# First token group read by whole rows, turned on TensorE, and scaled on two other engines

## The chip, the cores and the metric

The kernel runs on one core of a Trainium2 chip. Its time is the device time of one execution in microseconds, the median of several runs. Five engines work side by side and each takes its own instructions in order: TensorE (PE; PEld is its weight load), VectorE (DVE), ScalarE (ACT), GpSimd (POOL) and SyncE (SP), which here only issues transfers. An engine waits only where an instruction needs the result of another engine or of a transfer.

## The reference, cut to what matters

One layer of a mixer over 2048 tokens of 1024 features, all in float32. The part that the change touches is the entrance of the layer:

```python
shift, scale, gate = jnp.split(jax.nn.silu(c) @ w_ada[l] + b_ada[l], 3, axis=-1)
h = rms_norm(x) * (1.0 + scale[:, None, :]) + shift[:, None, :]
y = h @ w_in[l]          # then split into retention and attention heads and their gates
```

`rms_norm` divides each token by the root of the mean of its 1024 squares. `scale` and `shift` are one number per feature. So every token needs its own factor, every feature its own factor and offset, and the factor of a token is known only when all of its 1024 features have been squared and summed. What follows (retention over chunks of 128 tokens, windowed attention with a sink, gating, output projection, a last norm) is the same before and after.

## The kernel before, in words

The 2048 tokens go in four groups of 512 (`GT`), and group 3 is the first. The 1024 features are eight rows of 128 (`NK = 8`, index `k`): a row lies on the 128 partitions, the 512 tokens beside one another, so that a row is at once the moving operand of the input projection. Float32 operands are split into a rounded high part and the rest as a low part, and each product is three matmuls (high x high, high x low, low x high; `PASSES`).

**The head.** Group 3 comes from HBM already with features on the partitions (`x3`, four transfers from `xt`). ACT squares the eight rows (L990), DVE adds the squares (`add`, L985), and four small matmuls sum them over the partitions (`own_sums`, L982). ACT makes the mean (L184), POOL the power -1/2 (L185), DVE a diagonal of it (L192), and PE spreads the token factors over all partitions into a bank `ps3` (L201). Beside this the row of `c` is copied to all partitions by two matmuls (`pc0`, L968) and passed through silu on ACT (`silu0`, L971). `warm` (L962) issues matmuls whose result nobody reads.

**The conditioning.** For each row `k`, `ada` loads two blocks of `w_ada` (`wss`, 512 KB each), multiplies each by the silu row and sums it (`weigh`, L216, 128x1024 on DVE), and adds the bias (L227): that gives shift and scale of the 128 features (`mod`).

**The first loop.** It runs over `k` from 0 to 7. `start_load` brings two rows of four column chunks of `w_in` every second `k` (L1030); ACT rounds them to the high part (L112), DVE subtracts to get the low part (`start_low`, L1042). `modulate` makes the row: DVE multiplies by the scale and by the token factor (L232), ACT adds the shift and rounds (`h3h`, L233), DVE takes the low part (`h3l`, L234). Then PE does 4 chunks x 2 halves x 3 passes = 24 matmuls for this row (L1069), into eight banks that stay open over all eight rows. For rows 1 to 7 the token factors are read from `r3`, a copy of `ps3` in SBUF (L1057).

The order on each engine is fixed by the program where `keep_in_program_order` (`fixed`) is used, by `behind(i)` (an instruction is issued after `i`), and otherwise by a scheduler. The `wss` blocks go round five buffers, the raw weights and other loads round seven.

## Time and profile before

| what | value |
|---|---|
| median of 3 runs | 1138.04 us (1137.48 to 1139.66) |
| the profiled execution | 1139.05 us, span 1137.2 us |
| PE busy | 1120.9 us (99% of the span) |
| DVE busy | 800.0 us (70%) |
| ACT busy | 466.9 us (41%) |
| POOL busy | 328.5 us (29%) |
| first matmul of the first loop | 18.77 us after the span's start |
| first matmul behind the first loop | 64.00 us |

A row of the timeline gives start, length, engine, line, operation, the tiles written and read, and how many instructions were merged; in square brackets the idle time ahead of it and what ended it. A line number is that of the kernel before. The span is the time from the first to the last instruction; the execution lasts 1.85 us longer.

### The profile page before, as it was taken

What the parts mean: (1) busy time and instruction counts of PE and PEld (TensorE: products, weight loads), DVE (VectorE), ACT (ScalarE), POOL (GpSimd) and SP (SyncE); (2) the same over time, 40 slices, a digit from 0 to 9 for tenths busy, and PEclk for the clock granted to TensorE, in tenths of its full rate; (3) what the DMA queues carried; (4) which work ended last, traced back from release to release, by engine and by line L of the source; (5) the groups of instructions that cost most, each with busy time, mean ns of one, the idle gap of its engine ahead of it and who ended that gap; (6) DMA issues with size and microseconds to landing.
All of it is one profiled execution on the core that took longest, in us unless ns stands there. A gap on an engine that the chain in (4) does not pass through costs nothing.

```text
span 1137.2 us, 18696 instructions
## 1 busy us (share of the span) xinstructions
PE 1120.9 (99%) x6342; PEld 961.7 (85%) x6342; DVE 800.0 (70%) x2033; ACT 466.9 (41%) x1032; POOL 328.5 (29%) x427
## 2 busy tenths in 40 slices
PE   8999999999999999999999999999999999999997
PEld 5886889989988889998888887888888888888886
DVE  7973994565763645756658266888888888888885
ACT  4344522242452002322110155555555555555563
POOL 0000020110010200000204154555555555555552
PEclk9998999999999999999999999999999999999999
DMA  9948893374675542534347267466666666666531
GB/s 339 337 150 254 293 284 134 118 264 117 191 238 166 158 123 75 169 110 143 93 148 251 70 180 252 162 226 229 225 229 228 228 227 227 227 227 227 190 140 74
DMA packets 156246, 219.59 MB, mean 193 GB/s; under 512 B 13043, under 2 KB 105075, under 8 KB 156022
## 3 DMA queue, kind: packets, MB, share of 16 engines
q1 hardware_dynamic: 140020, 210.30, 56.4%
q10 hardware_dynamic: 16130, 8.09, 2.4%
q8 instruction: 50, 0.82, 0.3%
q14 instruction: 46, 0.38, 0.1%
HBM read 130.13 MB, written 50.86 MB: 159 GB/s over the span
## 4 chain that ended last, share of the span: by engine, by line
PE 84%; DVE 5%; issue 5%; DMA 2%; ACT 2%; POOL 1%; POOLq 0%; DVEq 0%; ACTq 0%
PE pz L1313 14%; PE rv L357 8%; PE rk L344 8%; PE ag L344 7%; PE o L1232 6%; PE aq L344 5%; PE rg L344 4%; PE S L769 4%; PE rq L344 4%; PE pt L1215 4%; PE S L773 2%; PE u L473 2%; PE av L344 2%; PE ak L344 2%; PE y L834 1%
## 5 line engine op out<-in xcount | busy, mean ns | idle before, releaser
L796 POOL TENSOR_SCALAR p<-p,m 128x640 f32<-128x640 f32 (+1 forms) x112 | 95.2, 850 | 86.1 <-DMA kwin<-d_k 46.4
L1222 DVE TENSOR_TENSOR phl<-pt,phl 128x512 fp32r<-128x512 f32 x154 | 104.7, 681 | 20.6 <-ACT phl L1221 20.5
L786 ACT ACTIVATE p<-p,m 128x641 f32<-128x641 f32 (+1 forms) x112 | 92.3, 824 | 62.2 <-DVE m L783 40.4
L1221 ACT ACTIVATE phl<-pt 128x512 fp32r<-128x512 f32 x154 | 90.9, 592 | 40.2 <-PE pt L1215 33.8
L1313 PE MATMUL pz<-wg0h,mr 128*128 128x512 f32 (+1 forms) x264 | 99.9, 402 | 0.7 <-DVE mr L114 0.7
L1313 PE MATMUL pz<-wg1h,ma 128*128 128x512 f32 x240 | 94.6, 414 | 0.0
L777 DVE CUSTOM_DVE_ANT_0 p<-S,msk 128x640 f32<-128x640 f32 (+1 forms) x112 | 90.1, 805 | 2.9 <-PE S L773 1.1
L769 PE MATMUL S<-kwin,aq 128*128 128x384 f32 (+1 forms) x256 | 84.9, 351 | 0.4 <-DVE m L777 0.4
L449 ACT ACTIVATE vw<-v,wdec 128x128 fp32r<-128x128 f32 x128 | 43.7, 394 | 84.3 <-DVE v L462 84.2
L1232 PE MATMUL o<-phl,vwin 128*128 128x512 f32 x180 | 72.1, 428 | 0.2 <-ACT phl L1221 0.2
L773 PE MATMUL S<-kctx,aq 128*128 128x256 f32 x256 | 71.1, 281 | 0.0
L1215 PEld LDWEIGHTS pt<-identr,pr 128*128 128x128 f32 x552 | 60.0, 141 | 11.6 <-DMA pr<-p 0.8
L1215 PE MATMUL pt<-identr,pr 128*128 128x128 f32 x552 | 63.0, 241 | 0.4 <-DMA pr<-p 0.4
L1313 PEld LDWEIGHTS pz<-wg0h,mr 128*128 128x128 f32 x264 | 49.2, 188 | 9.5 <-DVE mr L114 0.9
L769 PEld LDWEIGHTS S<-kwin,aq 128*128 128x128 f32 x256 | 48.1, 188 | 5.4 <-DVE m L777 1.8
L773 PEld LDWEIGHTS S<-kctx,aq 128*128 128x128 f32 x256 | 48.3, 189 | 3.1
L1313 PE MATMUL pz<-wg0l,mr 128*128 128x512 f32 (+1 forms) x132 | 50.9, 385 | 0.0
L1313 PEld LDWEIGHTS pz<-wg1h,ma 128*128 128x128 f32 x240 | 45.2, 188 | 5.2
L1313 PE MATMUL pz<-wg1l,ma 128*128 128x512 f32 x120 | 47.2, 393 | 0.0
L1277 ACT ACTIVATE ob<-o 64x512 f32<-64x512 f32 x32 | 19.0, 595 | 67.4 <-PE o L1232 67.4
L451 DVE SCALAR_TENSOR_TENSOR vw<-v,wdec,vw 128x128 fp32r<-128x128 f32 x128 | 39.9, 357 | 6.7 <-ACT vw L449 6.7
L1232 PE MATMUL o<-phl,vctx 128*128 128x512 f32 x128 | 43.9, 405 | 0.0
(456 smaller groups left out, 3116.5 us busy)
## 6 DMA issues: line engine op xcount, KB each, us to landing
pr<-p SPq DMA_DIRECT2D x104, 320.0 KB, 3.0
wss<-in_wss SPq DMA_DIRECT2D x32, 512.0 KB, 6.4
...
```

The lines of the kernel that those rows point to most:

```text
L344: pe.matmul(ps, w[:, a, k, c0 : c0 + P], ht[b][:, k, :], start=(k == 0 and i == 0), stop=(k == NK - 1 and i == 2),)
L357: pe.matmul(ps, ht[a][:, k, t * P : (t + 1) * P], w[:, b, k, :], start=(k == 0 and i == 0), stop=(k == NK - 1 and i == 2),)
L769: i = pe.matmul(psc[:, o:512].rearrange("p (s t) -> p s t", t=P), AQ[b][:, h, :], C2["kwin"][:, kv, hl, ksel], start=(hl == 0), stop=(hl = ...
L773: pe.matmul(psc[:, 512:768], AQ[b][:, h, :], C2["kctx"][:, kv, hl], start=(hl == 0), stop=(hl == 1))
L777: i = PE["max"] = dve.tensor_tensor_reduce(out=pb[:, 0:n], in0=psc[:, o : o + n], in1=mk, op0=ALU.add, op1=ALU.max, scale=1.0, scalar=-3e3 ...
L786: act.activation(pb[:, 0 : n + 1], pb[:, 0 : n + 1], AF.Exp, bias=m4[:, 1, j : j + 1], scale=0.125, accum_out=m4[:, 2, j : j + 1],)
L796: PE["norm"] = pool.tensor_scalar(pb[:, 0:n], pb[:, 0:n], m4[:, 2, j : j + 1], 0.0, op0=ALU.mult, op1=ALU.add)
L1215: pe.transpose(ppt[:, j].bitcast(F32R), x, identr)
L1221: PE["phl"] = act.activation(phl[0], ppt, AF.Copy)
L1222: PE["low"] = dve.tensor_tensor(phl[1], ppt, phl[0], op=ALU.subtract)
L1232: pe.matmul(PO[kv], vt, PH[kt][hl], start=(kt == 0 and hl == 0), stop=(kt == nkt - 1 and hl == 1))
L1313: PE["prod"] = pe.matmul(pz, m[:, a, k % RH, :], WG[k // 4][c][:, k % 4, s], start=(k == 0 and i == 0), stop=(k == NK - 1 and i == 2),)
```

## The change

Only the head and the first loop are written anew.

- **Load.** Group 3 is read as four blocks of 128 tokens by 1024 features (`xr`, from `xn`), 512 KB each as before. PE turns it: 32 transposes of 128x128 (`turn`), and ACT copies the eight turned banks into `x3` (`turned`).
- **Squares.** A token is now one partition, so a square and its sum are one instruction for a block of 128x1024 (`square`): two on ACT, two on DVE, all ahead of the two silus. The seven adds and the summing matmuls are gone.
- **The row of c** lies in a tile that DVE has cleared first, and is copied out by matmuls over 128 partitions where it was one.
- **Diagonal.** Half of it is made on DVE between the two `weigh` of row 0, half on ACT.
- **Row 0** (`first_row`) has its order written out. Its weights come as half pieces (`start_load(0, 0)` and `start_load(0, 1)`, 128 KB each), and the low part of chunk rg1 is made on POOL.
- **Rows 1 to 7** (`later_row`): POOL multiplies the row by the token factors in place, ACT applies scale and shift in one instruction, ACT rounds, DVE subtracts. One DVE instruction per row (L232) is gone and the other (L234) becomes a plain subtraction; POOL has one more per row and ACT one more.

On **POOL**, around the head and the first loop (r_x: the power of the token means; wrg: weights of chunk rg; h2x: the group `x3`; r: the token factors `r3`; half: constants). Before:

```order
masks.py:197 MEMSET ident 128x128
masks.py:199 ISA
masks.py:199 AFFINE_SELECT ident<-ident 128x128
L185 TENSOR_TENSOR r_x_212<-r_x_212,half_84 128x4
L185 TENSOR_TENSOR r_x_587<-r_x_587,half_84 128x4
L185 TENSOR_TENSOR r_xc<-r_xc,half_84 128x2
```

Now:

```order
masks.py:199 AFFINE_SELECT ident<-ident 128x128
L1012 TENSOR_TENSOR r_x_198<-r_x_198,half_84 128x4
L1059 TENSOR_TENSOR wrg_236<-wr_s_0_251,wrg_236 128x256
L1088 TENSOR_TENSOR h2x_132<-h2x_132,r_247 128x512 x7
L185 TENSOR_TENSOR r_x_615<-r_x_615,half_84 128x4
L185 TENSOR_TENSOR r_xc<-r_xc,half_84 128x2
```

Where POOL had nothing between the powers of two groups, it now has a subtraction and seven multiplications one behind the other.

On **DVE**, from the low part of row 0 to the conditioning of row 2 (wss: blocks of `w_ada`; wrg, w_srq: weights; h3h, h3l: the row's parts). Before:

```order
L234 SCALAR_TENSOR_TENSOR h3l<-h2x_125,mod,h3h 128x512
L1042 TENSOR_TENSOR wrg_232<-wr_s_0_246,wrg_232 128x512
L216 SCALAR_TENSOR_TENSOR wss_1_0_286,acc_113<-wss_1_0_286,row_123 128x1024
L216 SCALAR_TENSOR_TENSOR wss_1_1_289,acc_113<-wss_1_1_289,row_123 128x1024
L227 TENSOR_TENSOR mod<-acc_113,nbada 128x2
L232 SCALAR_TENSOR_TENSOR h2x_125<-h2x_125,mod,r_257 128x512
L216 SCALAR_TENSOR_TENSOR wss_2_0_320,acc_113<-wss_2_0_320,row_123 128x1024
L234 SCALAR_TENSOR_TENSOR h3l<-h2x_125,mod,h3h 128x512
L216 SCALAR_TENSOR_TENSOR wss_2_1_323,acc_113<-wss_2_1_323,row_123 128x1024
L1042 TENSOR_TENSOR wrg_231<-wr_s_1_327,wrg_231 128x512
L227 TENSOR_TENSOR mod<-acc_113,nbada 128x2
```

Now (after `h3l` of row 0 and the low part of rq0):

```order
L209 SCALAR_TENSOR_TENSOR wss_1_0_295,acc_113<-wss_1_0_295,row_123 128x1024
L1059 TENSOR_TENSOR w_srq_237<-wr_s_0_251,w_srq_237 128x256
L209 SCALAR_TENSOR_TENSOR wss_1_1_298,acc_113<-wss_1_1_298,row_123 128x1024
L222 TENSOR_TENSOR mod<-acc_113,nbada 128x2
L1059 TENSOR_TENSOR wrg_235<-wr_s_0_248,wrg_235 128x256
L1059 TENSOR_TENSOR w_srq_238<-wr_s_0_248,w_srq_238 128x256
L1091 TENSOR_TENSOR h3l<-h2x_132,h3h 128x512
L1059 TENSOR_TENSOR w_srq_237<-wr_s_0_251,w_srq_237 128x256
L1059 TENSOR_TENSOR wrg_236<-wr_s_0_251,wrg_236 128x256
L209 SCALAR_TENSOR_TENSOR wss_2_0_342,acc_113<-wss_2_0_342,row_123 128x1024
L209 SCALAR_TENSOR_TENSOR wss_2_1_345,acc_113<-wss_2_1_345,row_123 128x1024
L1059 TENSOR_TENSOR wrg_235<-wr_s_1_349,wrg_235 128x512
```

The scaling of row 1 has left DVE, the weights come in halves, and both blocks of row 2 stand behind the low parts of row 1, where the first of them stood ahead of `h3l` of row 1. The sum of row 2 (`mod`) follows the last row shown.

The diff, cut to its core:

```diff
-    act.dma_start(row0[0:1], crow[0:1])
+    xr = [ld.tile([P, D], F32, tag="ld", name=f"xr3_{t}") for t in range(4)]
+    for t in range(4):
+        nc.sync.dma_start(xr[t], xn[(12 + t) * P : (13 + t) * P, :])
     x3 = half("h2x3", [P, NK, GT], F32)
-    for i in range(4):
-        nc.sync.dma_start(x3[:, 2 * i : 2 * i + 2], xt[3][:, 2 * i : 2 * i + 2])
...
+    dve.memset(row0, 0.0)
+    act.dma_start(row0[0:1], crow[0:1])
...
+    def square(t, eng):
+        y, a = sq[t % 2], s3.ss[:, t : t + 1]
+        if eng == "act":
+            fixed(act.activation(y, xr[t], AF.Square, accum_out=a))
+        else:
+            fixed(dve.scalar_tensor_tensor(y, xr[t], 1.0, xr[t], op0=ALU.mult, op1=ALU.mult, accum_out=a))
+    def turn(t, ks):
+        for k in ks:
+            fixed(pe.transpose(xp[k][:, t * P : (t + 1) * P], xr[t][:, k * P : (k + 1) * P], ident))
+    def turned(*ks):
+        for k in ks:
+            PE["turned"] = fixed(act.activation(x3[:, k], xp[k], AF.Copy))
...
+    warm(6)
...
+    turn(0, range(6))
+    for n in range(2):
+        fixed(pe.matmul(pc0[n], ones, row0[:, n * GT : (n + 1) * GT], start=True, stop=True))
+    for t in range(1, 4):
+        turn(t, range(6))
+    square(0, "act")
+    square(1, "dve")
+    square(2, "act")
+    square(3, "dve")
     silu0(0)
     silu0(1)
+    for t in range(4):
+        turn(t, (6, 7))
...
+    turned(0, 1)
+    warm(5, ps3)
...
+    ada(
+        st0, "ada", row0, 0, 0, fix=fixed,
+        between=lambda: fixed(dve.tensor_tensor(dg[:, 0:2], i2, r2_, op=ALU.mult)),
+    )
+    for t in (2, 3):
+        fixed(act.activation(dg[:, t], ident, AF.Copy, scale=r[:, 0, t : t + 1]))
+    for t in range(4):
+        fixed(pe.matmul(ps3[:, t * P : (t + 1) * P], ones, dg[:, t], start=True, stop=True))
+    turned(2)
+    warm(8, pacc.tile([P, GT], F32, tag="acc", name="warm2"))
...
+    def first_row():
+        x, h = x3[:, 0], H[3]
+        shk, sck = mod[:, 0, 0, 0:1], mod[:, 0, 0, 1:2]
+        start_high(0, CH[:1], 0, 1, fixed)
+        turned(3)
+        start_high(0, CH[1:2], 0, 1, fixed)
+        PE["scaled"] = fixed(dve.scalar_tensor_tensor(x, x, sck, ps3, op0=ALU.mult, op1=ALU.mult))
+        start_low(0, CH[:1], 0, 1, fixed)
+        fixed(act.activation(h[0][:, 0, :], x, AF.Identity, bias=shk))
+        fixed(dve.scalar_tensor_tensor(h[1][:, 0, :], x, shk, h[0][:, 0, :], op0=ALU.add, op1=ALU.subtract))
+        start_low(0, CH[1:2], 0, 1, fixed)
+        lows = [PE["low0"]]
+        turned(6, 7)
+        start_high(0, CH[2:3], 0, 1, fixed)
+        start_low(0, CH[2:3], 0, 1, fixed)
+        fixed(act.activation(r3, ps3, AF.Copy))
+        start_high(0, CH[3:], 0, 1, fixed)
+        lows.append(PE["low0"])
+        start_low(0, CH[3:], 0, 1, eng=pool)
+        turned(4, 5)
+        return lows
+    def later_row(k):
+        x, h = x3[:, k], H[3]
+        with behind(plow):
+            pool.tensor_tensor(x, x, r3, op=ALU.mult)
+        act.activation(x, x, AF.Identity, bias=mod[:, k, 0, 0:1], scale=mod[:, k, 0, 1:2])
+        PE["hirow"] = act.activation(h[0][:, k, :], x, AF.Copy)
+        PE["row"] = dve.tensor_tensor(h[1][:, k, :], x, h[0][:, k, :], op=ALU.subtract)
...
     for k in range(NK):
-        if k:
-            ada(st0, "ada", row0, k, 0, (PE["scaled"],) * 2)
...
-        modulate(x3[:, k], r3 if k else ps3, 0, H[3], k)
...
+        if k == 0:
+            start_load(0, 0)
+            lows = first_row()
+        else:
+            cond = ada(st0, "ada", row0, k, 0, lows if k == 1 else (PE["row"],) * 2)
...
+            later_row(k)
```

More of the change, by code (lines that the diff above doesn't have):

```diff
@@ L219, in behind, with ada @@
         return tc.issue_after(i.ins) if i else nullcontext()
-    def ada(pl, tag, row, kc, which, after=(None, None)):
+    def ada(pl, tag, row, kc, which, after=(None, None), fix=lambda i: i, between=lambda: None):
         for j in range(2):
@@ L225, in ada @@
             with behind(after[j](i) if callable(after[j]) else after[j]):
-                i = weigh(w, row, acc2[:, kc, which, j : j + 1])
+                i = fix(weigh(w, row, acc2[:, kc, which, j : j + 1]))
+            if j == 0:
+                between()
         return dve.tensor_tensor(mod[:, kc, which], acc2[:, kc, which], nbada[:, kc:16:8], op=ALU.add)
@@ L964, in tile_hymba @@
     fixed = tc.keep_in_program_order
-    warm(12)
-    for n in range(2):
-        pc0[n] = ptp.tile([P, GT], F32, tag="tp", name=f"pc0{n}")
-        fixed(pe.matmul(pc0[n], ones[0:1], row0[0:1, n * GT : (n + 1) * GT], start=True, stop=True))
     def silu0(n):
@@ L973, in tile_hymba @@
     s3 = Stats(GT, "x3")
-    zero4 = rsm.tile([P, 4], F32, tag="zero", name="zero4", bufs=1)
-    dve.memset(zero4, 0.0)
-    s3.ss = ptp.tile([P, 4], F32, tag="tp", name="ss_x3")
-    fixed(pe.matmul(s3.ss, ones, zero4, start=True, stop=False))
-    def own_sums(x):
-        for t in range(4):
-            fixed(pe.matmul(s3.ss[:, t : t + 1], x[:, t * P : (t + 1) * P], ones[:, 0:1], start=False, stop=t == 3))
-    def add(x, y):
-        fixed(dve.tensor_tensor(x, x, y, op=ALU.add))
-    sq = [tmp(f"sq_x3_{k}") if k < 4 else ld.tile([P, GT], F32, tag="ld", name=f"sq_x3_{k}") for k in range(NK)]
@@ L989, in square @@
-    def square(k):
-        fixed(act.activation(sq[k], x3[:, k], AF.Square))
-    warm(12)
-    for i in range(2):
-        square(2 * i)
-        square(2 * i + 1)
-        add(sq[2 * i], sq[2 * i + 1])
-    add(sq[0], sq[2])
-    square(4)
-    square(5)
-    add(sq[4], sq[5])
-    add(sq[0], sq[4])
-    square(6)
+    s3.ss = rsm.tile([P, 4], F32, tag="ss", name="ss_x3")
+    def square(t, eng):
[4 more added lines that the diff above has]
+            fixed(dve.scalar_tensor_tensor(y, xr[t], 1.0, xr[t], op0=ALU.mult, op1=ALU.mult, accum_out=a))
@@ new lines, in turn @@
+    def turn(t, ks):
[4 more added lines that the diff above has]
+            PE["turned"] = fixed(act.activation(x3[:, k], xp[k], AF.Copy))
+    sq = half("h2sq", [P, 2, 2 * D], F32)[:, :, 0:D]
+    sq = [sq[:, i] for i in range(2)]
+    warm(6)
+    for n in range(2):
+        pc0[n] = ptp.tile([P, GT], F32, tag="tp", name=f"pc0{n}")
+    xp = [
+        (ptp if k > 4 else pacc).tile([P, GT], F32, tag="tp" if k > 4 else "acc", name=f"xp{k}") for k in range(NK)
+    ]
@@ L1003, in tile_hymba @@
+    turn(0, range(6))
+    for n in range(2):
+        fixed(pe.matmul(pc0[n], ones, row0[:, n * GT : (n + 1) * GT], start=True, stop=True))
[5 more added lines that the diff above has]
+    square(3, "dve")
     silu0(0)
-    square(7)
-    add(sq[0], sq[6])
     silu0(1)
-    add(sq[0], sq[7])
-    own_sums(sq[0])
-    warm(8)
-    s3.roots(ada(st0, "ada", row0, 0, 0))
-    ps3 = s3.spread()
-    warm(6)
+    for t in range(4):
+        turn(t, (6, 7))
```

72 lines of the change are left out of this document (42 added, 30 removed).

## The prediction

> **What bounds the kernel now.** I read the page's totals first, then the waits of PE in the first 75 us, then the timeline of each engine there.
>
> ```profile
> PE 1120.9 (99%) x6342; PEld 961.7 (85%) x6342; DVE 800.0 (70%) x2033; ACT 466.9 (41%) x1032; POOL 328.5 (29%) x427
> ...
> PE frg L1069 <- ACT h3h L233: 0.6, 2, 0.3
> PE aq L344 <- ACT g L604: 0.3, 1, 0.3
> ```
>
> PE is the bound of the whole, and once the first loop runs it hardly waits: 0.6 us for the parts of a row, 0.3 us ahead of the next projection. So the change can gain only by starting the loop sooner, and can lose by making PE wait inside it; both pass to the end one for one. The rows that set the start, and those that set row 2:
>
> ```profile
> 8.86 0.63 ACT L990 ACTIVATE sq_x<-h2x 128x512 f32<-128x512 f32 x1
> ...
> 11.92 1.22 DVE L216 SCALAR_TENSOR_TENSOR wss<-wss,row 128x1024 f32<-128x1024 f32 x1
> ...
> 13.20 0.27 ACT L184 ACTIVATE r_x<-ss_x,half 128x4 f32<-128x4 f32 x1 [2.08 <-PE ss_x L982]
> 13.55 1.63 POOL L185 TENSOR_TENSOR r_x<-r_x,half 128x4 f32<-128x4 f32 x1 [12.26 <-ACT r_x L184]
> 15.21 0.69 DVE L192 TENSOR_TENSOR dg_x<-ident,r_x 128x512 f32<-128x512 f32 x1 [0.72 <-POOL r_x L185]
> 16.05 1.13 PE L201 MATMUL rr_x<-dg_x,ones 128*128 128x128 f32 x8 [1.14 <-DVE dg_x L192]
> 17.22 0.75 DVE L232 SCALAR_TENSOR_TENSOR h2x<-h2x,mod,rr_x 128x512 f32<-128x512 f32 x1 [0.71 <-PE rr_x L201]
> 18.00 0.72 ACT L233 ACTIVATE h3h<-h2x,mod 128x512 fp32r<-128x512 f32 x1 [2.18 <-DVE h2x L232]
> 18.77 0.73 PE L1069 MATMUL frg<-h3h,wrg 128*128 128x512 f32 x2 [0.30 <-ACT h3h L233]
> ...
> 27.27 0.15 DVE L227 TENSOR_TENSOR mod<-acc,nbada 128x2 f32<-128x2 f32 x1
> 27.34 1.28 DVE L1042 TENSOR_TENSOR w_srq<-wr_s,w_srq 128x512 fp32r<-128x512 f32 x2
> 28.54 0.68 DVE L1042 TENSOR_TENSOR wrg<-wr_s,wrg 128x512 fp32r<-128x512 f32 x1
> ...
> 30.70 0.73 PE L1069 MATMUL frg<-h3h,wrg 128*128 128x512 f32 x2 [0.33 <-ACT h3h L233]
> ...
> 64.00 0.50 PE L344 MATMUL aq<-h3h,w_s 128*128 128x512 f32 x1 [0.29 <-ACT g L604]
> ```
>
> The loop's first matmul is at 18.77. The last quarter of the input is there by 8.86 (its first square starts then); the ten microseconds between are sums, mean, power, diagonal, spread, scaling. Rows 2 to 7 take 64.00 - 0.29 - 30.70 = 33.0 us, or 5.5 each: from row 2 on PE sets the pace.
>
> ```profile
> 18.77:25.00 6.23, 6.13 (x26) 4.78 (x27) 6.08 (x12) 1.61 (x4) 0.00 (x0) 1.00 1.00 367
> 25.00:31.00 6.00, 5.67 (x25) 4.37 (x24) 6.00 (x12) 2.36 (x5) 0.00 (x0) 1.00 0.96 322
> ```
>
> Columns: the stretch, its length, busy time of PE, PEld, DVE, ACT, POOL, PE clock, share and GB/s of DMA. While rows 0 and 1 run DVE has no gap (6.08 of 6.23, 6.00 of 6.00) and POOL does nothing. DVE is the near second; whatever holds it up in rows 0 to 2 reaches PE.
>
> **The change, part by part. The head.** The four blocks bring the same bytes, so I keep 8.86 for the last. On its square DVE spends what a `weigh` of the same shape takes, 1.22: sums at 10.1. ACT's mean 0.27: 10.4. POOL's power 1.63: 12.1. ACT makes half of the diagonal, two pieces of 0.39: 12.9, while DVE makes the other half between the two `weigh`. The spread ends with its last matmuls at 13.6 (1.13 for eight from 12.5, when DVE's half is there). DVE meanwhile does the second `weigh` (12.5 to 13.7) and the sum (13.9); then L1068 and ACT's rounding, 0.75 and 0.72: first matmul at 15.4, **3.4 us sooner**. Seven adds, the summing matmuls and two squares behind one another are what is saved.
>
> The rows for the diagonal, the SP issues and the transposes:
>
> ```profile
> L196 ACT ACTIVATE dg_x<-ident,r_x 128x128 f32<-128x128 f32 x4 | 1.3, 391 | 1.1 <-POOL r_x L185 1.1
> ...
> 5.26 1.75 SPq L1030 DMA_DIRECT2D wr_s<-in_win x4
> ...
> 284.97 0.82 PE L433 MATMUL pk<-ident,m_rk 128*128 128x128 f32 x6
> ...
> 5.79 1.98 PE L968 MATMUL pc<-row,ones 1*128 1x512 f32 x4
> ```
>
> Six transposes take 0.82, 0.11 from start to start, so the 14 behind the last block take 1.5 and are done by 10.4, ahead of the power; without that cover they would cost the 1.5. The two matmuls for the row of c (1.98) are due only when both of ACT's squares are done, near 8.7; the later transfer of that row can slip 0.6 before DVE, which waits for the power until 12.1, feels it. Half-size weight pieces mean four more issues on SP; the four of before took 1.75, so up to 1.8 of SP time, between nothing and that, and I take nothing, because the blocks of row 2 are not used until far later (below).
>
> **The loop.** Per row DVE loses L232 (0.75); ACT and POOL have room. But POOL now works while DVE does, and the trace has stretches where both do:
>
> ```profile
> 154.67 1.63 DVE L216 SCALAR_TENSOR_TENSOR wss<-wss,room 128x1024 f32<-128x1024 f32 x1
> 156.23 0.08 DVE L216 DVE_READ_ACCUMULATOR wss<-wss,room 128x1 f32 x1
> 156.23 0.56 DVE L227 TENSOR_TENSOR mod<-acc,nbada 128x2 f32<-128x2 f32 x1
> ...
> 153.90 5.25 POOL L110 TENSOR_SCALAR w_brk<-wr_brk 128x512 fp32r<-128x512 f32 x4 [53.17 <-DMA wr_brk<-in_win]
> ...
> 608.22 6.18 DVE L658 TENSOR_TENSOR wg0l<-wf,wg0h 128x512 fp32r<-128x512 f32 x6
> ...
> 601.46 9.34 POOL L110 TENSOR_SCALAR wg0h<-wf 128x512 fp32r<-128x512 f32 x8 [13.57 <-DVE wf L646]
> ...
> 808.52 2.09 DVE L1338 SCALAR_TENSOR_TENSOR xb<-xb,rz,fw 128x512 f32<-128x512 f32 x2
> ...
> 808.13 0.73 POOL L1284 TENSOR_TENSOR ma<-mf,ma 128x256 fp32r<-128x256 f32 x1
> 808.84 1.24 POOL L796 TENSOR_SCALAR p<-p,m 128x640 f32<-128x640 f32 x1
> ...
> L1284 POOL TENSOR_TENSOR ma<-mf,ma 128x256 fp32r<-128x256 f32 x32 | 23.4, 730 | 2.7
> L817 POOL TENSOR_TENSOR qd<-qkv,decq 128x512 f32<-128x512 f32 x30 | 38.1, 1291 | 0.0
> L110 POOL TENSOR_SCALAR w_ark<-wr_ark 128x512 fp32r<-128x512 f32 x8 | 4.7, 618 | 51.6 <-PE rk L344 33.9 <-PE rq L344 17.8
> ```
>
> The same `weigh` takes 1.63 instead of 1.22 and the same sum 0.56 instead of 0.15, both 0.41 more, while POOL rounds 128x512 beside them; POOL's four take 5.25, though one alone takes 0.62. Six subtractions beside POOL take 6.18, where alone they start 0.60 apart (27.34 to 28.54 is two). So a DVE instruction with two SBUF inputs and a POOL instruction exclude one another and take turns, and each POOL instruction costs a busy DVE its own time less some 0.2. Behind a two-input POOL instruction it is the same: the L1338 at 808.52 and the next need 2.09 for two, and the first cannot begin in earnest before the 0.73 from 808.13 is over.
>
> A POOL multiplication of two 128x512 tiles takes 1.29, so it holds DVE for about 1.09; that pairing of shapes is not in the trace. From below the price is 0.41 (the one-input rows), from above 1.29 (all of it); I take 1.09, since the 128x256 form held DVE to its end. The subtraction on POOL (0.73) holds 0.53. All eight run in rows 0 to 2, because the seven multiplications wait for nothing but turned rows: 7 x 1.09 + 0.53 = **8.2 us** laid on DVE.
>
> [...]
>
> DVE's own work from the first matmul to the sum of row 2, by the new order: `h3l` 0.66 and 0.61, four `weigh` at 1.14, six half subtractions at 0.34 (half of 0.60 and a little), one whole 0.61, two sums 0.1: 8.7. With 8.2 the sum of row 2 is at 16.9 behind the first matmul, and none of that hides in a wait: DVE reaches `h3l` of row 1 about 0.5 after ACT has the row ready. ACT's two instructions (0.6 each, with the hand-over 1.3) make row 2 ready at 18.2, that is 15.4 + 18.2 = 33.6, against 30.70: **2.9 later**. Three more subtractions (1.8) and `h3l` (0.68) stand ahead of the low part, at 19.4; PE wants it 0.45 after its start and waits **0.75**. By the same turn-taking row 1 is late too (ready at 6.6, low part at 9.0, PE done with it at 13.9), which leaves PE idle for 4.3 us ahead of row 2.
>
> ```profile
> 8.00:8.50 0.50, 0.50 (x3) 0.19 (x3) 0.47 (x2) 0.50 (x2) 0.00 (x0) 0.53 1.07 410
> ...
> 11.00:11.50 0.50, 0.50 (x3) 0.15 (x1) 0.40 (x2) 0.12 (x1) 0.00 (x0) 0.56 0.99 348
> ...
> 15.00:16.00 1.00, 0.00 (x0) 0.00 (x0) 0.79 (x2) 0.76 (x2) 0.18 (x1) 1.00 1.04 426
> ```
>
> That has a price of its own: behind the two microseconds of matmuls over one partition (L968, above) the granted clock was 0.53 and less from 8.0 to 11.5. An idle stretch of 4.3 should do the same: 3.4 us at half clock lose 1.7. Bounds: nothing (the 1.14 ahead of L201 left it at 1.00), and twice that; I take **1.7**. From row 3 on DVE has 9.7 per two rows (four `weigh`, two `h3l`, four subtractions, sums, one wait for ACT) against PE's 11.0: no further wait, and no catching up, since PE is full. The 0.3 ahead of aq goes, as ACT has more time there.
>
> Sum: 2.9 + 0.75 + 1.7 - 0.3 = 5.05 us. The profiled execution took 1139.05 (span 1137.2): 1144.1. It stood 1.0 above the median of 1138.04, so against the median **1143.1**.
>
> **The rivals.**
>
> *The two engines do not exclude each other for these forms.* Then row 2 is ready at 15.4 + 8.7 + 1.3 and a wait of 1.2 in row 1, near 26.7, 4.0 sooner: 1134. For it: POOL's 30 multiplications in L817 keep 1.29 each beside a DVE that is 70% busy. Against: most of DVE's work there reads PSUM, and every DVE instruction of this loop reads two SBUF tiles.
>
> *The hold is that of the one-input rows*, 8 x 0.41 = 3.3 instead of 8.2. Then row 2 is at 28.7, 2.0 sooner, with no gap long enough to cool PE: 1138.04 - 2.0 - 0.3, near 1136. Against: L1284.
>
> *PE is cold in the head.* The clock row above shows how little it takes. If it is at half clock from 8 on, the five `warm` and the spread (1.13, doubled) end 1.8 later, and everything hangs on the spread: 1144.9. For it: six `warm` fewer at the start. Against: the row of c now uses all 128 partitions. [...]
>
> **How the numbers follow.** Forecast 0.55, cold head 0.12, short hold 0.16, no exclusion 0.17. What this kernel's runs can tell from no change is about 0.2%, or 2.3 us: below 1135.8 is faster, above 1140.3 slower. No exclusion is faster; of the short hold half is, half the same; the forecast without the clock term and with a little less hold gives 1140, so 0.06 of it goes to the same. Faster 0.24, same 0.15, slower 0.61. The range leaves out most of the no-exclusion case below and, above, two windows of half clock on a cold head: 1135.5 to 1147. The forecast's own range is 1140 to 1146.
>
> **What would show it.** First matmul of the loop near 15.4. In rows 0 to 2, DVE subtractions of 128x256 near 1.4 and `weigh` near 2.3 beside seven POOL multiplications of 1.6 to 2.4 that end near 31. A PE wait of over 3 us ahead of row 2, then a clock below 1.00. Row 2 at 33.6, the projection aq at 69. It is wrong if POOL's seven take 1.29 each and DVE's lengths stay as they were, or if row 2 starts before 30.7.

## The result, and the profile after

The changed kernel takes 1143.93 us (median of 6 runs, 1143.51 to 1145.88) where the kernel before takes 1137.86 (6 runs beside it): a ratio of 1.0054, with a 95% interval of 1.0041 to 1.0067, or 6.1 us more. Its profiled execution took 1145.88, with a span of 1144.1 (before: 1139.05 and 1137.2).

The waits of TensorE in the first 90 us after the change (what waited, for what: us in total, how often, the longest):

```profile
PE frg L1128 <- ACT h3h L1090: 5.5, 2, 3.2
PE pc L998 <- DMA row<-in_crow: 2.0, 1, 2.0
...
PE aq L339 <- ACT g L599: 1.2, 1, 1.2
PE frg L1128 <- DVE h3l L1091: 1.1, 1, 1.1
```

The 0.6 us of waits for a row's parts became 6.6, the wait ahead of aq went from 0.3 to 1.2, and there is a new one in the head, 2.0 for the row of c. The head, in the timeline of TensorE:

```profile
7.55 3.10 PE L998 MATMUL pc<-row,ones 128*128 128x512 f32 x4 [2.03 <-DMA row<-in_crow]
10.44 3.58 PE L982 MATMUL xp<-ident,xr 128*128 128x128 f32 x26
13.87 1.24 PE L962 MATMUL rr_x<-wones 128*128 128x512 bf16 x5
14.94 1.05 PE L1024 MATMUL rr_x<-dg_x,ones 128*128 128x128 f32 x8
17.59 0.73 PE L1128 MATMUL frg<-h3h,wrg 128*128 128x512 f32 x2
```

The loop starts at 17.59, 1.18 sooner than before. The four matmuls of the row of c start late and take 3.10 us, and 26 transposes stand behind them in TensorE's fixed order. Then the loop, in the timelines of GpSimd, of VectorE and of TensorE:

```profile
19.69 0.74 POOL L1059 TENSOR_TENSOR wrg<-wr_s,wrg 128x256 fp32r<-128x256 f32 x1 [6.25 <-DMA wss<-in_wss]
20.39 11.16 POOL L1088 TENSOR_TENSOR h2x<-h2x,r 128x512 f32<-128x512 f32 x7
```

```profile
18.58 1.22 DVE L209 SCALAR_TENSOR_TENSOR wss<-wss,row 128x1024 f32<-128x1024 f32 x1
...
19.72 0.99 DVE L1059 TENSOR_TENSOR w_srq<-wr_s,w_srq 128x256 fp32r<-128x256 f32 x1
20.63 2.31 DVE L209 SCALAR_TENSOR_TENSOR wss<-wss,row 128x1024 f32<-128x1024 f32 x1
...
22.99 1.11 DVE L222 TENSOR_TENSOR mod<-acc,nbada 128x2 f32<-128x2 f32 x1
24.02 0.41 DVE L1059 TENSOR_TENSOR wrg<-wr_s,wrg 128x256 fp32r<-128x256 f32 x1
24.36 1.48 DVE L1059 TENSOR_TENSOR w_srq<-wr_s,w_srq 128x256 fp32r<-128x256 f32 x1
...
30.32 2.31 DVE L209 SCALAR_TENSOR_TENSOR wss<-wss,row 128x1024 f32<-128x1024 f32 x1
...
34.31 0.15 DVE L222 TENSOR_TENSOR mod<-acc,nbada 128x2 f32<-128x2 f32 x1
```

```profile
36.09 1.22 PE L1128 MATMUL frg<-h3h,wrg 128*128 128x512 f32 x2 [3.23 <-ACT h3h L1090]
71.54 0.50 PE L339 MATMUL aq<-h3h,w_s 128*128 128x512 f32 x1 [1.20 <-ACT g L599]
```

GpSimd's seven multiplications take 11.16, that is 1.59 apart where one alone takes 1.29. From 20.6 to 31.5 VectorE's `weigh` takes 2.31 instead of 1.22 and the little sum L222 1.11 instead of 0.15; once GpSimd is done it takes 0.15 again (34.31). Seven of VectorE's instructions there are lengthened, one for each multiplication; those of them that don't stand above are low parts. The small one at 24.02 is not (0.41, its length alone). Such a hold shows as a longer instruction and not as idle time in square brackets, so an engine can lose time in more ways than by waiting for a result. Row 2 starts at 36.09, which is 18.5 behind the loop's first matmul (before: 11.93), and aq at 71.54, 7.54 later than before. The stretches around row 2 (length, busy time of PE, PEld, DVE, ACT, POOL, granted clock, DMA share, GB/s):

```profile
30.00:34.00 4.00, 2.86 (x13) 2.05 (x11) 4.00 (x6) 0.00 (x0) 1.55 (x2) 1.00 0.09 22
34.00:36.00 2.00, 0.00 (x0) 0.00 (x0) 2.00 (x5) 1.41 (x2) 0.00 (x0) 0.88 0.89 296
36.00:38.00 2.00, 1.91 (x5) 1.54 (x6) 2.00 (x5) 0.04 (x1) 0.00 (x0) 0.50 0.82 181
38.00:40.00 2.00, 2.00 (x8) 1.63 (x7) 1.32 (x5) 0.55 (x1) 0.00 (x0) 0.77 1.01 363
```

Behind the gap TensorE's clock is at half from 36 to about 39 (0.50, then 0.77 over 38 to 40). And the loads nearly stop from 30 to 34 (share 0.09): SyncE, which issues them, waits 9.3 us in one piece there for VectorE to be done with a block of `wss`, since VectorE, held up, frees no buffers.

### The profile page after: what moved, and what is told of

It is laid out like the page before. It is cut to its first block, busy times and chain, and to the rows that moved or that the text cites. A ratio compares the mean times of both kernels' runs of the same rounds, so it can differ in the third digit from the quotient of the medians.

```text
span 1144.1 us, 18738 instructions
## 1 busy us (share of the span) xinstructions
PE 1119.2 (98%) x6344; PEld 963.1 (84%) x6345; DVE 802.2 (70%) x2026; ACT 474.6 (41%) x1049; POOL 342.3 (30%) x435
## 4 chain that ended last, share of the span: by engine, by line
PE 83%; DVE 5%; issue 4%; DMA 4%; POOL 2%; ACT 1%; SPq 0%; POOLq 0%; DVEq 0%; ACTq 0%
PE pz L1372 15%; PE rv L352 8%; PE rk L339 7%; PE ag L339 7%; PE o L1291 7%; PE aq L339 5%; PE rg L339 4%; PE S L764 4%; PE rq L339 4%; PE pt L1274 4%; PE S L768 2%; PE u L468 2%; PE av L339 2%; PE ak L339 2%; DVE wss L209 1%
## 5 line engine op out<-in xcount | busy, mean ns | idle before, releaser
L446 DVE SCALAR_TENSOR_TENSOR vw<-v,wdec,vw 128x128 fp32r<-128x128 f32 x128 | 40.0, 357 | 6.7 <-ACT vw L444 6.7
```

## The experiments

All eleven kernels start from the changed kernel unless the text says otherwise. Their milestones in the profiled executions, in us: the loop's first matmul; row 2's first matmul (with "about" where it waits for nothing and stands inside a joined row); the wait ahead of aq, and aq's first matmul; the span. The last column is the ratio to the kernel before on the same chip, with its 95% interval.

| kernel | loop | row 2 | wait, aq | span | ratio |
|---|---|---|---|---|---|
| before | 18.77 | 30.70 | 0.29, 64.00 | 1137.2 | |
| the change | 17.59 | 36.09 | 1.20, 71.54 | 1144.1 | 1.0054 (1.0041 to 1.0067) |
| loop part alone | 19.17 | about 37 | 1.41, 71.14 | 1142.8 | 1.0051 (1.0037 to 1.0065) |
| rows on VectorE | 18.68 | 32.05 | 0.63, 65.66 | 1137.1 | 0.9990 (0.9980 to 1.0000) |
| no multiplications | 16.07 | about 28 | 2.68, 63.81 | 1136.2 | 1.0004 (0.9993 to 1.0016) |
| one-input | 17.45 | 31.38 | 2.29, 66.66 | 1136.8 | 1.0007 (0.9992 to 1.0022) |
| spaced | 17.28 | about 30.3 | 2.38, 68.13 | 1140.0 | 1.0018 (1.0007 to 1.0029) |
| row of c early | 15.62 | 28.99 | 0.55, 62.50 | 1137.0 | 0.9993 (0.9983 to 1.0002) |
| fillers | 16.05 | 29.42 | 0.28, 62.73 | 1134.4 | 0.9985 (0.9976 to 0.9994) |
| no mult., late x | 16.03 | about 28 | 1.97, 62.92 | 1138.5 | 0.9985 (0.9973 to 0.9997) |
| early row, late x | 16.09 | 29.47 | none, 62.31 | 1140.6 | 1.0007 (0.9990 to 1.0024) |
| scale first | 16.18 | about 28 | 1.54, 62.99 | 1134.7 | 0.9981 (0.9971 to 0.9990) |
| round on GpSimd | 15.90 | about 28 | none, 61.02 | 1131.0 | 0.9941 (0.9928 to 0.9955) |

**Which part costs.** First the loop's part alone, put into the kernel before:

```diff
-        modulate(x3[:, k], r3 if k else ps3, 0, H[3], k)
+        if k:
+            x = x3[:, k]
+            pool.tensor_tensor(x, x, r3, op=ALU.mult)
+            act.activation(x, x, AF.Identity, bias=mod[:, k, 0, 0:1], scale=mod[:, k, 0, 1:2])
+            act.activation(H[3][0][:, k, :], x, AF.Copy)
+            PE["scaled"] = dve.tensor_tensor(H[3][1][:, k, :], x, H[3][0][:, k, :], op=ALU.subtract)
+        else:
+            modulate(x3[:, k], ps3, 0, H[3], k)
```

> The kernel before with one part of the change alone: rows 1 to 7 multiplied on GpSimd, scaled and rounded on ScalarE, with the remainder on VectorE. The head, the loads and whole weights are those of the kernel before, so no half of the weights is on GpSimd. My theory (this part is the whole loss): GpSimd's seven multiplications take 10.5 to 11.5 us in a line, VectorE's operations beside them are held 1.0 to 1.1 us each, row 2 starts 16.5 to 19 us behind the first matmul of the loop (11.93 in the kernel before), and the whole is 5 to 8 us over the kernel before, 1143.5 to 1147. The rival (the loss needs the split halves of the weights and the new order of the head): row 2 under 14 us behind, and the whole less than 3 us over the kernel before.

Measured: 1143.94 us, as much as the whole change. In the timelines of GpSimd, VectorE and TensorE of this kernel:

```profile
19.68 11.96 POOL L1055 TENSOR_TENSOR h2x<-h2x,r 128x512 f32<-128x512 f32 x7 [4.10 <-ACT r L1064]
```

```profile
20.15 1.78 DVE L1042 TENSOR_TENSOR wrg<-wr_s,wrg 128x512 fp32r<-128x512 f32 x1
21.85 2.31 DVE L216 SCALAR_TENSOR_TENSOR wss<-wss,row 128x1024 f32<-128x1024 f32 x1
```

```profile
29.14 1.22 PE L1076 MATMUL frg<-h3h,wrg 128*128 128x512 f32 x2 [4.23 <-ACT h3h L1057]
```

The holds are the same (1.09 for the low part and for the `weigh`), in a kernel with whole weights and the old head; GpSimd's seven take 11.96, a little over the theory's 11.5, and here the long gap stands ahead of row 1. Row 2 follows about 18 behind the first matmul. The rival falls: the loss needs neither the head nor the halves. The opposite kernel keeps the head and gives the rows back to VectorE:

```diff
-        x, h = x3[:, k], H[3]
-        with behind(plow):
-            pool.tensor_tensor(x, x, r3, op=ALU.mult)
-        act.activation(x, x, AF.Identity, bias=mod[:, k, 0, 0:1], scale=mod[:, k, 0, 1:2])
-        PE["hirow"] = act.activation(h[0][:, k, :], x, AF.Copy)
-        PE["row"] = dve.tensor_tensor(h[1][:, k, :], x, h[0][:, k, :], op=ALU.subtract)
+        PE["row"] = modulate(x3[:, k], r3, 0, H[3], k)
+        PE["hirow"] = PE["high"]
...
-            cond = ada(st0, "ada", row0, k, 0, lows if k == 1 else (PE["row"],) * 2)
+            cond = ada(st0, "ada", row0, k, 0, lows if k == 1 else (PE["scaled"],) * 2)
```

> The kernel after the change with later rows scaled as in the kernel before: one VectorE operation with both factors, then the rounding and the remainder; the first token group's whole-row loads, the turning by TensorE, the squares ahead of the silus and the split halves stay. My theory (the head of the change is worth its 1.18 us, the loop's part is the whole loss): first matmul of the loop near 17.6, row 2 11.5 to 13 us behind it, the whole 1136 to 1137.5, about 1.2 less than before. The rival (the head also costs something later: its halves of the weights on GpSimd, and the late order of loads): row 2 starts over 14 us behind the first matmul, and the whole is 1139 or more.

Measured: 1137.63, just over the theory's range, and 1.1 us under the kernel before by the ratio, near the 1.2 of the theory, though the interval reaches 1; the rows were 13.4 apart from the first matmul to row 2, a little over its 13, and this execution's loop began late, at 18.68 (see the head). So the loss is the loop's part, and the rest of the change is worth about a microsecond, with 0 to 2.3 in its interval.

**What holds VectorE.** Three kernels change the multiplications alone. Without them:

```diff
-        with behind(plow):
-            pool.tensor_tensor(x, x, r3, op=ALU.mult)
```

> The kernel after the change without the seven multiplications of later rows by the token factor on GpSimd (L1088); rows 1 to 7 are therefore computed without that factor. ScalarE's scaling, its rounding and VectorE's remainder stay as they are. My theory (the multiplications hold VectorE's two-input operations 1.07 to 1.11 us each and push the condition of row 2 back): VectorE's condition sum of row 1 (L222) takes 0.15 us and not 1.11, its weigh (L209) 1.22 and not 2.31, row 2's first matmul starts 11.0 to 13.0 us after the first matmul of the loop (18.5 after the change, 11.93 before), TensorE's clock stays at 1.00 from 34 us on, and the whole takes 1135.5 to 1138, no longer than the kernel before. The rival (ScalarE's two steps, L1089 and L1090, in the place of one VectorE step, or the weights being split in halves, make the wait): row 2 still starts more than 16 us after the first matmul, and the whole stays at 1141 to 1144.

VectorE's timeline in this kernel:

```profile
19.11 1.21 DVE L209 SCALAR_TENSOR_TENSOR wss<-wss,row 128x1024 f32<-128x1024 f32 x1
...
20.36 0.16 DVE L222 TENSOR_TENSOR mod<-acc,nbada 128x2 f32<-128x2 f32 x1
```

Every sign of the multiplications' hold is gone, and row 2 starts some 12 us behind the first matmul, as in the kernel before: ScalarE's two steps and the halves do not make that wait, and the rival falls. But the whole is not the 1135.5 to 1138 of the theory. The median is 1139.56, with a ratio that cannot be told from 1. Row 2 is about 2.5 us sooner than in the kernel before and aq only 0.19 sooner. The theory's clock of 1.00 from 34 us on was missed too. Both are followed up below.

One input in place of two, in the same seven places:

```diff
-            pool.tensor_tensor(x, x, r3, op=ALU.mult)
+            pool.tensor_scalar(x, x, 1.0, 0.0, op0=ALU.mult, op1=ALU.add)
```

> The kernel after the change with each of the seven multiplications on GpSimd replaced by an operation of the same shape and place that reads one tensor only (times 1 plus 0), so rows 1 to 7 lack the token factor. My theory (VectorE is held for as long as GpSimd's instruction runs, less about 0.2 us, so a shorter instruction holds it less: the one-input operation of 128x512 on GpSimd should take 0.6 to 0.8 us alone): VectorE's two-input operations beside it are held 0.3 to 0.6 us, not 1.07 to 1.11, row 2 starts 13 to 15.5 us behind the first matmul, and the whole takes 1137.5 to 1140. The rival (only operations in which both engines read two tensors exclude each other): VectorE's operations beside it show no hold at all, row 2 as without the multiplications, 1135.5 to 1137.5. A third way (GpSimd's one-input operation is no shorter, and holds as long): 1142 to 1144.5.

GpSimd's row, and VectorE beside it:

```profile
20.25 6.27 POOL L1088 TENSOR_SCALAR h2x<-h2x 128x512 f32<-128x512 f32 x7
```

```profile
20.49 1.63 DVE L209 SCALAR_TENSOR_TENSOR wss<-wss,row 128x1024 f32<-128x1024 f32 x1
...
22.16 0.45 DVE L222 TENSOR_TENSOR mod<-acc,nbada 128x2 f32<-128x2 f32 x1
22.86 0.82 DVE L1059 TENSOR_TENSOR w_srq<-wr_s,w_srq 128x256 fp32r<-128x256 f32 x1
```

The same VectorE instructions in the same places are held 0.41, 0.30 and 0.40, not 1.09, 0.96 and 1.07. GpSimd's one-input form of this shape takes 0.62 alone in this program (L110, in the prediction). So the hold goes with the length of GpSimd's instruction: 0.41 is 0.21 less than 0.62, and 1.09 is 0.20 less than 1.29. The half subtraction on GpSimd, two inputs and 0.74, lies between them: the low part beside it (at 19.72 in the changed kernel) takes 0.57 more. The whole, 1139.51, is in the theory's range. The rival's (no hold) and the third way's are excluded by these rows.

The same seven multiplications, one for each row:

```diff
-            pool.tensor_tensor(x, x, r3, op=ALU.mult)
+            fixed(pool.tensor_scalar(late[:, k : k + 1], mod[:, k - 1, 0, 0:1], 1.0, 0.0, op0=ALU.mult, op1=ALU.add))
+            fixed(pool.tensor_tensor(x, x, r3, op=ALU.mult))
```

> The kernel after the change, its seven multiplications on GpSimd kept, but each behind a tiny GpSimd operation that reads the modulation of the row before (128x1), so that they come one for each row and not seven in a line. My theory (what costs is seven in a line, 11.16 us in which VectorE gets every second turn): at most two of VectorE's operations between the first matmul and row 2 are held, by 1.07 to 1.11 us each, row 2 starts 12.5 to 15 us behind the first matmul, and the whole takes 1137 to 1140. The rival (it is the work on GpSimd that costs, wherever it stands, since each multiplication holds one operation of VectorE in any case): VectorE's delay is only spread, each row is late by about 1.1 us, and the whole is 1142 to 1144.5.

Measured: 1140.43, just over the theory's range and far from the rival's. Row 2 starts about 13 behind the first matmul. Some four of the 6.1 us go away with nothing removed, by spacing alone. What is left are single holds (the sum of row 1 takes 1.13, one low part 1.77) and a wait of 2.38 ahead of aq.

**The head.** The kernel with the rows on VectorE began its loop 1.1 us later than the changed kernel, with the same head. The row-of-c matmuls explain it. Their start, their length and the loop's first matmul in ten executions:

| kernel | start | length | loop | loop less start |
|---|---|---|---|---|
| no multiplications | 7.36 | 1.96 | 16.07 | 8.71 |
| no mult., late x | 7.40 | 1.96 | 16.03 | 8.63 |
| the change | 7.55 | 3.10 | 17.59 | 10.04 |
| spaced | 7.23 | 3.02 | 17.28 | 10.05 |
| one-input | 7.41 | 3.09 | 17.45 | 10.04 |
| rows on VectorE | 7.36 | 3.75 | 18.68 | 11.32 |
| fillers, first execution | 7.46 | 1.95 | 15.82 | 8.36 |
| fillers, timed | 7.69 | 1.95 | 16.05 | 8.36 |
| scale first | 7.48 | 1.95 | 16.18 | 8.70 |
| round on GpSimd | 7.42 | 1.95 | 15.90 | 8.48 |

TensorE's own queue sets the start: the row of c, the transposes behind it, the spread. If the clock falls behind the gap ahead of the row, the loop is 1.4 to 2.7 us later. In the changed kernel the granted clock shows it (0.50 from 8.5 to 11.5), and over 4 to 10 us it reads 0.83 in spaced and 0.84 in one-input, against 1.00 without the multiplications; with the rows on VectorE the matmuls are longer still and the transposes behind them take 4.21 and not 3.00, though the record there reads 1.00, and for that execution I go by the lengths. Two kernels close the gap. Both have the rows on VectorE. One fetches the row first:

```diff
+    act.dma_start(row0[0:1], crow[0:1])
     xr = [ld.tile([P, D], F32, tag="ld", name=f"xr3_{t}") for t in range(4)]
...
-    dve.memset(row0, 0.0)
-    act.dma_start(row0[0:1], crow[0:1])
...
-        fixed(pe.matmul(pc0[n], ones, row0[:, n * GT : (n + 1) * GT], start=True, stop=True))
+        fixed(pe.matmul(pc0[n], ones[0:1], row0[0:1, n * GT : (n + 1) * GT], start=True, stop=True))
```

> The previous edit (later rows on VectorE as in the kernel before) and, beside it, the row of c fetched first on ScalarE's queue, ahead of the table load and without the zero fill, and spread by a matmul that reads the one row alone, as in the kernel before. My theory (the head gained 1.18 us and not 3.4 because the row of c came at 7.2 to 7.6 us, after a gap in which TensorE's clock fell to half): the row's four matmuls start before 6.3 us and take 1.9 to 2.1 us (3.0 to 3.75 at half clock in four of the five traces with the late row, 1.96 in the fifth), the mean's power on GpSimd starts by 10.9, and the first matmul of the loop starts at 15.6 to 16.6. For the whole there are two answers. If what the loop gains at its start lasts, 1135.0 to 1136.3. If the loads bind the end of the loop (they fill the queues 0.97 to 1.02 from 20 to 60 us), the first matmul behind the loop waits 1.5 to 2.5 us for ScalarE's gate and the whole is 1136.5 to 1137.8, as without this edit. The second is the likelier.

The other fills the gap:

```diff
     turn(0, range(6))
+    warm(5, pc0[0])
     for n in range(2):
```

> Later rows on VectorE as in the kernel before, and five filler matmuls behind the first turned block, ahead of the matmuls of the row of c, in the gap of 1.2 to 2.0 us in which TensorE had nothing. My theory (the gap is what lets the clock fall): the row's four matmuls take 1.9 to 2.1 us, and the first matmul of the loop starts at 16.0 to 17.2. The rival (the clock falls at that place for another reason, so that filling the gap changes nothing): the four matmuls take 3.0 to 3.8 us, and the loop starts at 17.3 to 18.7.

> The kernel with later rows on VectorE and five fillers ahead of the matmuls of the row of c, now timed. In its one look TensorE's clock stayed at 1.00, the loop began at 15.82 us and the first matmul behind it (aq) at 62.52. My theory (1.5 us sooner at aq, of which a little is lost to the weights of the context's keys and values, whose waits grew by 0.2 us): 1136.0 to 1137.2, 1.2 to 2.4 less than the kernel before. The rival (what the start gains is taken back further on): within 0.7 us of the kernel before.

TensorE's timeline of the two, the early row first, then the fillers (first execution):

```profile
6.15 2.06 PE L996 MATMUL pc<-row,ones 1*128 1x512 f32 x4
...
15.62 0.74 PE L1122 MATMUL frg<-h3h,wrg 128*128 128x512 f32 x2
```

```profile
7.46 1.95 PE L999 MATMUL pc<-row,ones 128*128 128x512 f32 x4 [0.57 <-DMA row<-in_crow]
...
15.82 0.73 PE L1125 MATMUL frg<-h3h,wrg 128*128 128x512 f32 x2
```

Both start the loop where the theory said, the fillers 0.2 us sooner still, and in all four traces with fillers the row's matmuls took 1.95, where four of six without them took 3.0 to 3.75. In the early row's trace the row's matmuls took 2.06 and the clock stayed at 1.00. So it is the gap, and not the place, that lets the clock fall, in some executions and not in others, and the head of the change could have been worth 2.6 to 3 us. With fillers the whole took 1136.38, in the theory's range. With the early row it took 1138.23, 0.43 over the likelier of its two ranges, and not by the wait that was expected: aq waited 0.55 and started at 62.50, 1.5 sooner than before. The time went later, into waits for VectorE's low parts of the context's weights and of the weighted values:

```profile
158.07 5.29 PE L352 MATMUL crk<-w_brk,hc 128*128 128x256 f32 x41 [2.26 <-DVE w_brk L325]
166.70 1.34 PE L352 MATMUL crv<-w_brv,hc 128*128 128x256 f32 x9 [1.49 <-DVE w_brv L325]
```

In the kernel before the first of the two waits was not there, nor the 1.4 us in three waits for the low parts of the weighted values (vw, L446). At the second wait's end this execution is still 2.16 ahead of the kernel before (166.70 against 168.86); the rest is lost behind it. Why it is 2.26 here and 0.44 and 1.17 with fillers, whose loop starts 0.2 and 0.4 us later, is open.

**The end of the loop.** Why did aq not follow row 2 in the kernel without multiplications? ScalarE's timeline there, and TensorE's:

```profile
57.33 1.04 ACT L180 ACTIVATE xr_x<-xr_x 128x1024 f32<-128x1024 f32 x1
...
59.92 1.28 ACT L189 ACTIVATE dg_x<-ident,r_x 128x128 f32<-128x128 f32 x4 [1.13 <-POOL r_x L185]
61.11 2.17 ACT L112 ACTIVATE w_s<-wr_s 128x512 fp32r<-128x512 f32 x4
63.19 1.05 ACT L599 ACTIVATE g<-frg 128x512 f32<-128x512 f32 x2
```

```profile
63.81 0.51 PE L339 MATMUL aq<-h3h,w_s 128*128 128x512 f32 x1 [2.68 <-ACT g L599]
```

From the last of the four squares on, ScalarE has a fixed chain: mean, GpSimd's power, diagonals, four roundings of aq's weights, gate. aq follows the start of that square by 6.48; in the changed kernel by 6.49 (65.05 to 71.54), in the kernel before, too, by 6.49 (57.51 to 64.00). Here are the same squares in the kernel before and, with VectorE's sum of row 7 in each, after the change:

```profile
53.82 0.16 DVE L227 TENSOR_TENSOR mod<-acc,nbada 128x2 f32<-128x2 f32 x1
57.51 1.04 ACT L180 ACTIVATE xr_x<-xr_x 128x1024 f32<-128x1024 f32 x1
```

```profile
60.42 0.16 DVE L222 TENSOR_TENSOR mod<-acc,nbada 128x2 f32<-128x2 f32 x1
65.05 1.04 ACT L180 ACTIVATE xr_x<-xr_x 128x1024 f32<-128x1024 f32 x1
```

Without the multiplications, the clock behind the gap of 2.68 is at 0.58 from 64 to 66 and at 0.57 from 66 to 68, a further loss of some 1.7 us: the context's sums (L172) come at 100.47, 1.42 later than in the kernel before (99.05). What makes the square late? The first test moves loads:

```diff
-            xk2 = load_x(xt[2], GT, "x2")
...
     wa = load_w("aq0", "s", hi="act")
+    xk2 = load_x(xt[2], GT, "x2")
```

> The kernel without the seven multiplications (rows 1 to 7 lack the token factor) and, beside it, the four loads of the second token group (512 KB each, L150) issued behind the rows for its squares and the next weights, not ahead of the condition's weights of row 7. Without this edit row 2 started 2.5 us sooner than in the kernel before, and the first matmul behind the loop (aq, L339) only 0.19 us sooner, since it waited 2.68 us for ScalarE's gate. My theory (the wait comes from the loads: at some 370 GB/s the 2 MB are 5.7 us of the queue ahead of row 7's weights): VectorE's weigh of row 7 no longer waits for its weights, the squares come earlier, aq waits under 1.0 us and starts 45.0 to 46.7 us behind the first matmul of the loop (47.74 without the edit), and the whole falls by 1 to 2.4 us from 1139.56, to 1137.2 to 1138.6. The rival (ScalarE's own steps at the end of the loop make the wait, whenever the loads land): aq still waits over 2.0 us, and the whole is within 0.7 us of 1139.56.

ScalarE's timeline of this kernel, around row 7:

```profile
52.28 0.80 ACT L1087 ACTIVATE h2x<-h2x,mod 128x512 f32<-128x512 f32 x1
...
56.41 1.06 ACT L180 ACTIVATE xr_x<-xr_x 128x1024 f32<-128x1024 f32 x1 [2.67 <-DMA xr_x<-in_xn]
```

The answer lies between the two. VectorE's weigh of row 7 no longer waits, three squares move ahead of row 7, and the whole falls 1.95 us to 1137.61, in the theory's range (the execution shown is the slowest of its ten, at 1140.27). But the fourth square still waits 2.67 for its rows, whose load was issued late, and aq waits 1.97, not under 1.0, and hardly less than the rival's 2.0. The loads are part of it; moving these four does not settle it. With the rows on VectorE, the early row and this same move:

> Three edits together: later rows on VectorE as in the kernel before, the row of c fetched early, and the four loads of the second token group behind the next weights. Nothing of the computation is left out. My theory (a sooner start of the loop is worth something only if the loads at its end come sooner too): the first matmul of the loop at 15.6 to 16.6, aq waits under 1.0 us behind the loop and starts 46 to 47.5 us behind the loop's first matmul, and the whole is 1134.6 to 1136.2, 2 to 3.5 us less than the kernel before. The rival (the second group's loads, now late, hold its first row up, and the time comes back behind the first matmuls of aq): aq early, but TensorE waits for the second group's rows some 10 us later, and the whole is 1136.5 to 1138.

aq came at 62.31 without any wait, as the theory said, and the whole was 1137.79, as the rival said, in a wide spread (1135.94 to 1144.65). In the execution profiled, which took 1142.34, TensorE's waits stand neither at aq nor at the second group's rows but, as with the early row, at the context's weights, in its timeline:

```profile
160.08 5.24 PE L352 MATMUL crk<-w_brk,hc 128*128 128x256 f32 x41 [1.56 <-DVE w_brk L325]
...
169.16 2.08 PE L352 MATMUL crv<-w_brv,hc 128*128 128x256 f32 x9 [2.21 <-DVE w_brv L325]
```

Next, on top of the fillers, the scaling of a row ahead of the low parts of its weights, in rows 1, 2, 4 and 6:

```diff
-                with behind(cond):
-                    start_low(0, CH[:2], 1, 2)
...
-                with behind(PE["row"]):
-                    start_low(k // 2, CH)
             later_row(k)
+            if k % 2 == 0:
+                with behind(PE["scaled"]):
+                    start_low(k // 2, CH)
             if k == 1:
+                with behind(PE["scaled"]):
+                    start_low(0, CH[:2], 1, 2)
```

> The same with one more edit: VectorE scales rows 1, 2, 4 and 6 directly behind their conditions, and takes the low parts of the weights after that, where it took two to four of them ahead of the scaling. Nothing of the computation is left out. My theory: TensorE's waits for the rounded rows 1 and 2 (0.78 and 1.03 us) fall under 0.4 each, but the first matmul behind the loop gains at most 0.5 of it, since the loads bind the end of the loop: aq starts at 61.8 to 62.6 with a wait of 1 to 2 us, and the whole takes 1135.8 to 1137.2. The rival (the loop's end follows its rows): aq starts 1.2 to 1.8 us sooner, at 60.7 to 61.3, and the whole takes 1134.3 to 1135.6. A third way (the low parts are late now): TensorE waits for them in rows 1 and 2, and nothing is gained.

The waits for the rounded rows fell from 1.8 to 0.5 in all, and aq started at 62.99, 0.26 later than with fillers alone and 0.4 later than the theory's latest, its wait at 1.54. The whole, 1136.57, is in the theory's range and that of the fillers: 1.3 us saved in the loop, and nothing of it left at its end. The last kernel adds to this one a shorter chain:

```diff
-    wa = load_w("aq0", "s", hi="act")
+    wa = load_w("aq0", "s", hi="pool")
```

> The edits of the previous kernel (rows on VectorE, fillers, scaling ahead of the low parts) and one more: the weights of aq are rounded on GpSimd and not on ScalarE, so that ScalarE goes from the diagonals straight to the gate. Nothing of the computation is left out. In eleven of the twelve traces so far, with and without the change, aq's first matmul starts 6.48 to 6.51 us after the start of the fourth square of the second token group on ScalarE (the twelfth had no wait there); the four roundings are 2.08 us of that. My theory (ScalarE's chain from the fourth square to the gate is what aq waits for): aq starts 4.4 to 5.6 us after the fourth square, at 61.9 to 62.3 (62.99 without the edit), with a wait of 0.4 to 0.8 us and not 1.54, and the whole takes 1135.4 to 1136.4 (1136.57 without). The rival (GpSimd's roundings come later than ScalarE's did, after its power, and VectorE's low parts behind them): TensorE waits for aq's weights in place of the gate, aq's first matmul 6.0 us or more after the fourth square, and the whole is 1136.6 to 1138.

ScalarE's timeline of this kernel, and TensorE's:

```profile
56.22 1.06 ACT L180 ACTIVATE xr_x<-xr_x 128x1024 f32<-128x1024 f32 x1
...
58.83 1.28 ACT L189 ACTIVATE dg_x<-ident,r_x 128x128 f32<-128x128 f32 x4 [1.13 <-POOL r_x L185]
60.01 1.05 ACT L599 ACTIVATE g<-frg 128x512 f32<-128x512 f32 x2
```

```profile
61.02 0.39 PE L339 MATMUL aq<-h3h,w_s 128*128 128x512 f32 x1
```

aq follows the fourth square by 4.80 and waits for nothing: ScalarE's chain was what it had waited for. The whole is 1132.74 us, a ratio of 0.9941: it beats the kernel before by 6 us in the medians and the changed one by some 11. That is more than the theory gave, 1135.4 to 1136.4 with aq at 61.9 to 62.3. aq is 1.97 sooner than without the edit, the context's sums (L172) 2.59 sooner, the span 3.7. Of the last 1.1 the cause is open; the time from the context's values (crv) to the end lies between 965.9 and 971.4 in all these traces, whatever was changed.

## Why the prediction was right in its time, and where its steps were not

The forecast, 1143.1 within 1135.5 to 1147, held, and so did its mechanism; that it came within 0.8 us is in part luck, since errors of its terms cancelled (below). Its sum against the measured steps, each as a difference to the kernel before up to aq:

| step | predicted | measured |
|---|---|---|
| first matmul of the loop | -3.4 (at 15.4) | -1.18 (at 17.59) |
| row 2 behind the first matmul | 18.2 | 18.5 |
| row 2 | +2.9 | +5.39 |
| low part of row 2 | +0.75 | 0 |
| clock behind the gap | +1.7 | +1.25 |
| wait ahead of aq | -0.3 | +0.9 |
| sum at aq | +5.05 | +7.54 |

The clock's 1.25 is what is left of 35.45, the time from row 2 to aq, less 33.3 before and less 0.9; the stretch of the kernel before from which the 1.7 was taken lasts 3.4 us (0.50 from 8.0 to 11.4) and reads 0.50 to 0.56 in the prediction's rows, not "0.53 and less". That idle time would do the same was the author's estimate; in the changed kernel 3.23 us of it were followed by a clock of 0.50 (36 to 38). Behind aq 0.6 comes back (span +6.9), and the medians differ by 6.1.

*The exclusion* was right, in kind and in size: 1.09 forecast, 0.96 to 1.10 measured, 0.57 for GpSimd's half subtraction against 0.53. With seven holds VectorE's sum of row 2 ends 16.87 behind the first matmul, where 16.9 was forecast. Taking 0.41 beside 0.62 and stretching it to 1.29 less 0.2 is what the one-input run bears out. In these runs the hold is some 0.2 us shorter than the length of GpSimd's instruction alone, for 1.29 (1.09) and for 0.62 (0.41) alike.

*The head* was mis-sized, by 2.2 us. The step that failed is that the later transfer of the row of c "can slip 0.6 before DVE" feels it. VectorE was not the one to feel it. TensorE was, with 26 transposes queued behind those matmuls, and ScalarE, whose mean stood behind the second silu: it ran at 11.18 and not 10.1. And the transposes, costed at nothing because the power would cover them, ended (14.0) behind the power (13.44). The rival of the cold head had named the half clock, with fewer `warm` as its reason. That is borne out in part: behind the gap ahead of the row of c the clock fell (0.50 from 8.5 to 11.5), and five of them put there kept it up (1.00 from 6 to 14 with fillers, timed). The transposes do not bring it down by themselves: with fillers the same 26 take 3.00 at a clock of 1.00. Nor do the matmuls over one partition bring the clock down by themselves, as the prediction read its rows: in the early row's trace they take 2.06 and the clock stays at 1.00 behind them. Why one gap is followed by a slower TensorE and another is not, these runs do not settle: behind gaps of 1.24 and 2.03 the row's matmuls took 3.75 and 3.10, behind gaps of 1.26 and 1.42 they took 1.96, and behind one of 2.29 (one-input, ahead of aq) the clock read 1.00 (64 to 70 us).

*The wait ahead of aq* had the wrong sign. The step that failed is that it "goes, as ACT has more time there". ScalarE's last three squares stand behind the rounding of row 7, and that hangs on VectorE's sum of row 7. VectorE was 7.04 late at the sum of row 2 (34.31 against 27.27), more than TensorE was at row 2, and still 6.60 late at that of row 7 (60.42 against 53.82); ScalarE's two instructions for the row, with a square between them, added 1.04 more. So the fourth square came 7.54 late, and aq with it, where TensorE by itself was 6.63 late.

Behind this is a wrong premise, that what the start gains or loses passes "to the end one for one". A gain passes only as far as ScalarE's chain comes sooner too: in the kernel before that chain was ready 0.29 after TensorE. With fillers 1.28 at row 2 became 1.27 at aq; without the multiplications about 2.5 became 0.19. So the rivals' times were wrong as well: no exclusion at all was priced at 1134, and the kernel without multiplications, which comes nearest to it, with its row 2 at about 28, took 1139.56.

*The low part* cost nothing at row 2. It was there 0.78 behind the row's first matmul, and TensorE wanted it only behind five matmuls of high parts, 2.30 after its start (1.26 in the kernel before, at full clock) and not 0.45; in row 1, which the sum had left to the gap, it cost 1.13. These errors, +2.5 for row 2 and +1.2 for aq against -0.75 and -0.45, are in all 2.5 at aq. Two things took most of it back, and neither was foreseen: the 0.6 behind aq, and the median, which lies 1.95 under the profiled execution here and was taken as 1.0 under it. (Of its chances, faster should be 0.25 and the same 0.14 by its own working, not 0.24 and 0.15.)
